# Decay sums by broadcast transfers and GpSimd masks instead of matmuls, in a two-layer SSD / RG-LRU trunk

## The chip, the cores and the metric

The kernel runs on one core of a Trainium2 chip. The metric is the device time of one execution in microseconds (us), as a median of several runs; lower is better. One of the executions is also profiled, and its trace is what the rows below are read from. Engines are named as the profile names them: PE is the matmul engine (PEld its weight loads), DVE the vector engine, ACT the scalar engine, POOL is GpSimd, and SP issues the transfers (DMAs).

## The reference, cut to what matters

Two layers, 256 tokens, width 2048. Layer 0 has an SSD mixer, layer 1 an RG-LRU mixer; each is followed by a SwiGLU block and a gated input block. The change is inside the SSD mixer: 64 heads in 8 groups, two chunks of 128 tokens.

```python
dt = softplus(dt + dt_bias)                 # (256, 64)
a_cs = cumsum(dt * a, within a chunk)       # the decay sums
seg = a_cs[l] - a_cs[s]
decay_in = exp(where(l >= s, seg, -inf))    # (128, 128) per head and chunk
cb = C @ B.T                                # per group and chunk
y_diag = (cb * decay_in) @ (xs * dt)
# the state that chunk 0 hands to chunk 1 adds
# C[l] . B[s] * exp(a_cs1[l] + a_cs0[end] - a_cs0[s]) for l in chunk 1, s in chunk 0
```

For each head the kernel needs three 128x128 blocks of exponentials: chunk 0 on itself, chunk 1 on chunk 0, and chunk 1 on itself. Row s of a block holds the sum at token l along the free axis, less the sum at s, and the two diagonal blocks are masked to l >= s.

## The kernel before, in words

All products run as split products in fp32r: a weight tile `raw` is split by ACT into `hi` (L238) and by DVE into `lo` (L239), and each activation tile holds its own hi and lo side by side in 512 columns. A **panel** (`panel`) makes 512 output rows in four PSUM banks: 16 k-steps, taken in four **quarters** of four k-steps. A quarter is 16 matmuls of 512 columns (L266, weight `hi`) and then 16 of 256 columns (L264, weight `lo`). One load of 512 KB brings two k-steps, so a panel has eight loads, issued by SP (L230) in program order into five `raw` buffers; `hi` and `lo` have four buffers each, so ACT and DVE work at most four loads ahead of PE.

Small work is written as generators that a panel advances while it goes: `post` by one step for each k-step, `side` by `pump` steps. The order in which instructions then stand on each engine is set at build time; nothing is chosen while the kernel runs.

The SSD mixer's panels stand in this order: 18, 19 (C), the rates' panel `w_dt` (one quarter's work: 16 hi and 16 lo), 16, 17 (B), 8 to 15 (the eight groups' xs), 0 to 7 (z). The normalizing factor `r` comes from `bc_part(2)` while panel 19 runs (L186, L212 on PE). `dt_part` computes softplus (L356 to L370, a chain on DVE), the sums `cs` by scans (L412), and four transposes of them (L423). `group(g)` runs while the next panel runs: scaled (L162), convolution (ACT L349, DVE L351) and SiLU to `xs`; the C-by-B product (L444, L445) and its copy `cm`; transposes of `xs` to `xdt` (L454, L456); then for each of 8 heads two matmuls that spread the masked sums over the partitions (L468 the mask, L470 the sums), two exponentials on ACT (called at L473 and L474, recorded under L98), a product with `cm` on DVE (L475); then 16 matmuls that give the outputs (L487, L489) and `y` (L493). GpSimd runs only in the setup (L80, L82).

Of the kernel before, what the change touches and what calls it, by code (L numbers as in the profile page):

```python
# [11 lines left out]
F32 = mybir.dt.float32  # L12
F32R = mybir.dt.float32r
I32 = mybir.dt.int32
AF = mybir.ActivationFunctionType
# [10 lines left out]
KG = 2  # L26
RUN = 16
# [15 lines left out]
class Trunk:  # L43
# [7 lines left out]
    def __init__(self, ctx, tc):  # L51
        self.tc, self.nc = tc, tc.nc
        nc = self.nc
        pool = lambda name, bufs, **kw: ctx.enter_context(tc.tile_pool(name=name, bufs=bufs, **kw))
        self.const = pool("const", 1)
        self.act = pool("act", 48)
        self.wraw = pool("wraw", 5)
        self.wsp = pool("wsp", 4)
        self.tmp = pool("tmp", 2)
        self.ssd = pool("ssd", 2)  # L60
        self.ps = pool("ps", 8, space=bass.MemoryType.PSUM)
# [8 lines left out]
        self.identr = c.tile([P, P], F32R, name="identr")  # L70
        nc.vector.tensor_copy(self.identr, self.ident)
        self.sel = c.tile([P, 64], F32R, name="sel")
        nc.vector.tensor_tensor(self.sel, self.ident[:, :64], self.ident[:, 64:], ALU.add)
# [5 lines left out]
        mask = self.act.tile([P, 256], F32, name="mask", tag="a")  # L79
        nc.gpsimd.memset(mask, 0.0)  # L80
        for o in (0, P):
            nc.gpsimd.affine_select(  # L82
                out=mask[:, o:o + P], in_=mask[:, o:o + P],
                compare_op=ALU.is_ge, fill=-1e30, base=0, pattern=[[1, P]], channel_multiplier=-1)
        self.mask = c.tile([P, 256], F32R, name="maskr")
        nc.vector.tensor_copy(self.mask, mask)
        self.vecs = c.tile([P, NVEC], F32, name="vecs")
        self.h = c.tile([P, KT, T], F32, name="h")
# [7 lines left out]
    def table(self, out, in_, func, **kw):  # L96

        i = self.nc.scalar.activation(out, in_, func, **kw).ins  # L98
        if self.last_table is not None:
            self.tc.add_manual_dep(  # L100
                i, self.last_table.name,
                mybir.DependencyInfo(mybir.DependencyClass.NoSync, mybir.DependencyReason.DATA),
                reason="table order")
        self.last_table = i

# [116 lines left out]
    def weights(self, w, width=PW, kt=KG, also=None, single=False):  # L222
# [6 lines left out]
        if not single:  # L229
            nc.sync.dma_start(raw, w)  # L230
# [142 lines left out]
    def ssd_mixer(self, w_dt, w_in, w_out, load):  # L373
# [5 lines left out]

        def conv_silu(j, t, out):  # L380
            c = self.tmp.tile([P, T], F32, name="c", tag="c", bufs=3)
            self.conv(t, "ssd_cw", "ssd_cb", 48, j, c)
            self.table(out, c, AF.Silu)
# [14 lines left out]
        def dt_part(t):  # L398
# [23 lines left out]
            for i, src in enumerate((dt[:, :P], dt[:, P:], cs[:, :P], cs[:, P:256])):  # L422
                nc.tensor.transpose(b[:, i * P:(i + 1) * P], src, self.ident)  # L423
# [4 lines left out]
            self.csr, self.dts, self.ncs = csr, dts, ncs  # L428
            yield

        def of0(t):

            return t[:, :384].rearrange("p (a b) -> p a b", a=3)[:, 0:3:2, :]

        def group(g, ts):
            xs = [self.act.tile([P, 2, T], F32, name=f"xs{i}", tag="a") for i in range(2)]
            xs = [t[:, i, :] for t in xs for i in range(2)]
            for j, t in enumerate(ts):
                conv_silu(g * NB + j, self.scaled(t, self.r), xs[j])
                yield  # L440
# [3 lines left out]
            nc.tensor.matmul(of0(b), bt[:, :P], ct, start=True, stop=True, skip_group_check=True)  # L444
            nc.tensor.matmul(b[:, P:256], bt[:, P:], ct[:, P:], start=False, stop=True, skip_group_check=True)  # L445
# [4 lines left out]
            for c in range(2):  # L450
                yield
# [8 lines left out]
            yield  # L460
            es = []

            def decays(j):

                for hh in range(2):
                    hd = g * 8 + j * 2 + hh
                    rb = self.bank()
                    nc.tensor.matmul(rb[:, :256], self.identr, self.mask, start=True, stop=False,  # L468
                                     skip_group_check=True)
                    nc.tensor.matmul(rb[:, :384], self.sel[:, hd:hd + 1].to_broadcast([P, P]), self.csr,  # L470
                                     start=False, stop=True, skip_group_check=True)
                    e = pool.tile([P, 384], F32, name="e", tag="e", bufs=12)
                    self.table(of0(e), of0(rb), AF.Exp, bias=self.ncs[:, 0, hd:hd + 1])  # L473
                    self.table(e[:, P:256], rb[:, P:256], AF.Exp, bias=self.ncs[:, 1, hd:hd + 1])  # L474
                    nc.vector.tensor_tensor(e, e, cm, ALU.mult)  # L475
                    es.append(e)
                    yield

            def outputs(j):

                yb = self.bank()
                for i in (j, j + 1):
                    for hh in range(2):
                        e = es[i * 2 + hh]
                        ch = slice(i * P + hh * 64, i * P + hh * 64 + 64)
                        o = yb[hh * 64:hh * 64 + 64, (i - j) * T:(i - j + 1) * T]
                        nc.tensor.matmul(o, xdt[0][:, ch], of0(e), start=i == j, stop=False,  # L487
                                         skip_group_check=True)
                        nc.tensor.matmul(o[:, P:256], xdt[1][:, ch], e[:, P:256], start=False, stop=True,  # L489
# [51 lines left out]
        for g in range(8):  # L541
            banks = self.panel(w_in[g], u)
            self.post.append(gated(g, self.totals(banks)))
# [292 lines left out]
```

## Time and profile before

| | before |
|---|---|
| median of 3 runs | 2688.74 us (2687.94 to 2689.76) |
| profiled execution, its own time | 2686.82 us |
| its span in the trace | 2685.0 us |
| PE busy | 2663.3 us (99%) |
| PEld busy | 2348.0 us (87%) |
| DVE busy | 1821.1 us (68%) |
| ACT busy | 1497.8 us (56%) |
| POOL busy | 1.4 us (0%) |
| granted PE clock, mean | 0.998 |

The profiled execution's own time is 1.8 us above its span and 1.9 us below the median. Matmuls are pipelined, so the busy time of one is longer than the distance to the next; the distance between starts is what a matmul costs. The eight groups' stretch lies between about 132 and 360 us of the span.

### The profile page before, as it was taken

The page shows a single profiled execution, that of the slowest core. Times are in us where ns is not written, and L with a number is a line of the kernel's source. Part 1 is how long each engine was busy: PE and PEld are TensorE (multiplying, and loading weights), DVE is VectorE, ACT ScalarE, POOL GpSimd, SP SyncE. Part 2 cuts the span into 40 slices and gives each one's busy share as a digit, 9 for nine tenths or more (in the row PEclk, how much of TensorE's full clock was granted, in tenths as well). Part 3 has the DMA queues.
Part 4 walks back from the last instruction along what each step waited for, and adds up shares of the span by engine and source line. Part 5 has one row for each costly group of instructions (what it writes and reads, how often), then busy time and mean ns, then how long its engine had stood idle before and what let it go on. Part 6 is the DMA issues. An engine that isn't in the chain of part 4 may idle for free.

```text
span 2685.0 us, 40694 instructions
## 1 busy us (share of the span) xinstructions
PE 2663.3 (99%) x15474; PEld 2348.0 (87%) x15474; DVE 1821.1 (68%) x3101; ACT 1497.8 (56%) x2399; POOL 1.4 (0%) x9
## 2 busy tenths in 40 slices
PE   9999999999999999999999999999999999999998
PEld 7888888888888888888888888888888888888887
DVE  8888788855565555555666899977666555665667
ACT  7677666644444444444455678856444444444555
POOL 0000000000000000000000000000000000000000
PEclk9999999999999999999999999999999999999999
DMA  6544455555555555555555556555555555556553
GB/s 234 187 157 145 139 170 181 182 190 184 193 189 189 189 187 188 195 190 189 194 187 184 185 181 195 183 187 197 189 188 188 192 190 184 189 192 199 186 187 127
DMA packets 137140, 495.24 MB, mean 184 GB/s; under 512 B 15344, under 2 KB 15728, under 8 KB 136944
## 3 DMA queue, kind: packets, MB, share of 16 engines
q1 hardware_dynamic: 136944, 492.65, 55.5%
q8 instruction: 121, 1.98, 0.3%
q14 instruction: 75, 0.61, 0.1%
HBM read 490.49 MB, written 2.10 MB: 183 GB/s over the span
## 4 chain that ended last, share of the span: by engine, by line
PE 95%; DVE 3%; ACT 1%; issue 0%; DMA 0%; SPq 0%; DVEq 0%; ACTq 0%
PE bank L266 60%; PE bank L264 31%; DVE lo L239 1%; PE bank L487 1%; PE bank L581 1%; DVE c L351 0%; PE bank L470 0%; ACT hi L238 0%; PE bank L454 0%; PE bank L468 0%; DVE t L155 0%; PE bank L583 0%; PE bank L489 0%; DMA raw<-in_w_ssd_in_dram 0%; DVE xc L351 0%
## 5 line engine op out<-in xcount | busy, mean ns | idle before, releaser
L266 PE MATMUL bank<-x,hi 128*128 128x512 f32 x7360 | 1776.1, 392 | 6.3 <-ACT hi L238 5.5
L266 PEld LDWEIGHTS bank<-x,hi 128*128 128x128 f32 x7360 | 1350.8, 189 | 266.1 <-ACT hi L238 6.4
L238 ACT CAST hi<-raw 128x1024 fp32r<-128x1024 f32 (+1 forms) x932 | 973.0, 1048 | 1035.5 <-PE bank L266 984.6
L239 DVE TENSOR_TENSOR lo<-raw,hi 128x1024 fp32r<-128x1024 f32 (+1 forms) x932 | 1108.1, 1220 | 506.1 <-issue 419.6
L264 PEld LDWEIGHTS bank<-x,lo 128*128 128x128 f32 x7360 | 950.1, 191 | 39.5 <-DVE lo L239 2.5
L264 PE MATMUL bank<-x,lo 128*128 128x256 f32 x7360 | 969.7, 283 | 1.7 <-DVE lo L239 1.6
L155 DVE TENSOR_TENSOR t<-bank,s 128x256 f32<-128x256 f32 x448 | 161.7, 418 | 294.5 <-ACT s L152 294.2
L152 ACT COPY s<-bank 128x256 f32<-128x256 f32 x496 | 160.1, 374 | 12.6 <-PE bank L583 5.5
L162 DVE TENSOR_TENSOR t<-t,r 128x256 f32<-128x256 f32 x216 | 81.4, 420 | 0.0
L351 DVE SCALAR_TENSOR_TENSOR c<-t,vecs,c 128x255 f32<-128x255 f32 (+2 forms) x144 | 61.7, 481 | 1.3 <-ACT c L349 1.3
L144 ACT ACTIVATE x<-h,vecs 128x256 fp32r<-128x256 f32 x96 | 47.4, 501 | 16.8 <-DVE h L332 13.8
L98 ACT ACT_TABLE_LOAD x41 | 52.6, 1283 | 4.6 <-DVE c L351 4.0
L332 DVE TENSOR_TENSOR h<-h,t 128x256 f32<-128x256 f32 x144 | 54.2, 421 | 0.2
L145 DVE SCALAR_TENSOR_TENSOR x<-h,vecs,x 128x256 fp32r<-128x256 f32 x96 | 45.6, 481 | 5.6 <-ACT x L144 5.6
L98 ACT ACTIVATE e<-bank,ncs 128x256 f32<-128x256 f32 (+1 forms) x128 | 44.4, 423 | 5.9 <-PE bank L470 5.3
L175 DVE TENSOR_TENSOR acc<-acc,q 128x256 f32<-128x256 f32 x104 | 43.8, 421 | 3.1 <-ACT q L168 1.8
L168 ACT ACTIVATE q<-h 128x256 f32<-128x256 f32 x104 | 41.5, 405 | 5.6 <-DVE h L332 3.8
L98 ACT ACTIVATE sg<-t 128x256 f32<-128x256 f32 x88 | 32.3, 413 | 18.7 <-DVE t L162 18.7
L136 ACT CAST x<-t 128x256 fp32r<-128x256 f32 x88 | 31.8, 403 | 18.7 <-DVE t L673 18.7
L475 DVE TENSOR_TENSOR e<-e,cm 128x384 f32<-128x384 f32 x64 | 33.4, 554 | 3.7 <-ACT e L98 3.6
L349 ACT ACTIVATE c<-t,vecs 128x256 f32<-128x256 f32 x48 | 26.4, 592 | 13.2 <-DVE t L162 13.1
L137 DVE TENSOR_TENSOR x<-t,x 128x256 fp32r<-128x256 f32 x88 | 33.3, 421 | 0.0
(129 smaller groups left out, 719.5 us busy)
## 6 DMA issues: line engine op xcount, KB each, us to landing
raw<-in_w_ffn_in_dram SPq DMA_DIRECT2D x352, 512.0 KB, 4.4
raw<-in_w_ffn_out_dram SPq DMA_DIRECT2D x176, 512.0 KB, 4.4
raw<-in_w_ssd_in_dram SPq DMA_DIRECT2D x158, 512.0 KB, 4.3
raw<-in_w_ssd_out_dram SPq DMA_DIRECT2D x64, 512.0 KB, 4.4
raw<-in_w_ple_gate_dram SPq DMA_DIRECT2D x64, 512.0 KB, 4.2
raw<-in_w_lru_in_dram SPq DMA_DIRECT2D x64, 512.0 KB, 4.4
raw<-in_w_lru_out_dram SPq DMA_DIRECT2D x32, 512.0 KB, 4.4
raw<-in_w_ple_up_dram SPq DMA_DIRECT2D x8, 512.0 KB, 4.9
```

Of the source, the lines that this page charges most:

```text
L98: i = self.nc.scalar.activation(out, in_, func, **kw).ins
L144: nc.scalar.activation(x[:, :T], src, AF.Copy, scale=w)
L145: nc.vector.scalar_tensor_tensor(x[:, T:], src, w, x[:, :T].bitcast(F32), ALU.mult, ALU.subtract)
L152: nc.scalar.copy(s, b[:, T:])
L155: nc.vector.tensor_tensor(t, b[:, :T], s, ALU.add)
L162: self.nc.vector.tensor_tensor(t, t, r, ALU.mult)
L238: self.last_hi = nc.scalar.copy(hi, src).ins
L239: nc.vector.tensor_tensor(lo, src, hi.bitcast(F32), ALU.subtract)
L264: nc.tensor.matmul(b[:, T:], wt, x[:, :T], start=False, stop=k == nk - 1, skip_group_check=True)
L266: nc.tensor.matmul(b, wt, x, start=k == 0, stop=False, skip_group_check=True)
L332: self.nc.vector.tensor_tensor(hb, hb, t, ALU.add)
L351: nc.vector.scalar_tensor_tensor(out[:, d:], t[:, :T - d], self.vec(cw, (3 - d) * ntap + i), out[:, d:], ALU.mult, ALU.add)
```

## The change

The matmuls that spread the sums over partitions go, with the constants made for them (`identr`, `sel`, `mask`, `csr`). In their place the sums `cs` of all heads are written once to DRAM in 8 copies (`sums`), and for each pair of heads one transfer reads 768 values of a copy into all 128 partitions of a tile `e` (16 partitions read the same copy). Two GpSimd instructions then put -1e30 where l < s in the diagonal blocks, and the exponentials run in place on that tile. `move` puts each of these transfers into SP's queue behind the weight load issued last. One product with `cm` covers two heads. The three blocks of a head lie in another order in the tile. The rates' panel runs second instead of third, `dt_part` is pumped at 0.6 instead of 0.3, and a group's exponentials for two pairs of heads are written ahead of the transposes.

```diff
+    def move(self, out, in_):
+        i = self.nc.sync.dma_start(out, in_).ins
+        self.tc.add_manual_dep(
+            i, self.last_load.name, ...,
+            reason="place in the queue")
...
-            nc.sync.dma_start(raw, w)
+            self.last_load = nc.sync.dma_start(raw, w).ins
...
+        sums = self.dram.tile([NCOPY, 64, 384], F32, name="sums")
...
-            for c in range(2):
-                nc.vector.tensor_tensor_scan(cs[:, c * P:(c + 1) * P], self.ones, adt[:, c * P:(c + 1) * P],
+            for c, o in ((0, 0), (1, 256)):
+                nc.vector.tensor_tensor_scan(cs[:, o:o + P], self.ones, adt[:, c * P:(c + 1) * P],
                                              0.0, ALU.mult, ALU.add)
-            nc.vector.tensor_scalar(cs[:, 256:], cs[:, P:256], cs[:, P - 1:P], None, ALU.add)
-            csr = pool.tile([P, 384], F32R, name="csr", tag="csr", bufs=1)
-            nc.scalar.copy(csr, cs)
-            nc.vector.tensor_tensor(csr[64:, :], cs[64:, :], csr[64:, :].bitcast(F32), ALU.subtract)
+            nc.vector.tensor_scalar(cs[:, P:256], cs[:, 256:], cs[:, P - 1:P], None, ALU.add)
...
+            self.move(sums.rearrange("n h c -> h n c"), cs[:64].unsqueeze(1).to_broadcast([64, NCOPY, 384]))
+            yield
...
             for j, t in enumerate(ts):
                 conv_silu(g * NB + j, self.scaled(t, self.r), xs[j])
+                e = pool.tile([P, 2, 384], F32, name="e", tag="e", bufs=8)
+                hd = g * 8 + 2 * j
+                src = sums[0, hd:hd + 2, :]
+                self.move(e.rearrange("p h c -> p (h c)"),
+                          bass.AP(src.tensor, src.offset, [[64 * 384, NCOPY], [0, P // NCOPY], [1, 768]]))
+                for o in (0, 256):
+                    nc.gpsimd.affine_select(
+                        out=e[:, :, o:o + P], in_=e[:, :, o:o + P], compare_op=ALU.is_ge, fill=-1e30,
+                        base=0, pattern=[[0, 2], [1, P]], channel_multiplier=-1)
+                es.append(e)
                 yield
...
+            def decays(j):
+                e = es[j]
+                for hh in range(2):
+                    hd = g * 8 + j * 2 + hh
+                    self.table(e[:, hh, :256], e[:, hh, :256], AF.Exp, bias=self.ncs[:, 0, hd:hd + 1])
+                    self.table(e[:, hh, 256:], e[:, hh, 256:], AF.Exp, bias=self.ncs[:, 1, hd:hd + 1])
+                    yield
+                nc.vector.tensor_tensor(e, e, cm.unsqueeze(1).to_broadcast([P, 2, 384]), ALU.mult)
...
-                for hh in range(2):
-                    hd = g * 8 + j * 2 + hh
-                    rb = self.bank()
-                    nc.tensor.matmul(rb[:, :256], self.identr, self.mask, start=True, stop=False,
-                                     skip_group_check=True)
-                    nc.tensor.matmul(rb[:, :384], self.sel[:, hd:hd + 1].to_broadcast([P, P]), self.csr,
-                                     start=False, stop=True, skip_group_check=True)
-                    e = pool.tile([P, 384], F32, name="e", tag="e", bufs=12)
-                    self.table(of0(e), of0(rb), AF.Exp, bias=self.ncs[:, 0, hd:hd + 1])
-                    self.table(e[:, P:256], rb[:, P:256], AF.Exp, bias=self.ncs[:, 1, hd:hd + 1])
-                    nc.vector.tensor_tensor(e, e, cm, ALU.mult)
...
             yield from decays(0)
             yield from decays(1)
+            tokens(0)
             yield from decays(2)
+            tokens(1)
             yield from decays(3)
+            yield
             yield
...
         ts = self.totals(self.panel(w_in[18], u, pre=load))
         self.post.append(bc_part(2, ts, self.last_hi))
+        dt = self.totals(self.panel(w_dt, u, kt=8, nb=1, post=False))
         ts = self.totals(self.panel(w_in[19], u))
         self.post.append(bc_part(3, ts))
-        ts = self.totals(self.panel(w_dt, u, kt=8, nb=1, post=False))
-        self.side.append(dt_part(ts[0]))
+        self.side.append(dt_part(dt[0]))
         for n in (0, 1):
-            ts = self.totals(self.panel(w_in[16 + n], u, pump=0.3))
+            ts = self.totals(self.panel(w_in[16 + n], u, pump=0.6))
```

How the instructions stand is shown at three places. First PE where the rates' transposes stand, before. The L266 and L264 rows are quarters of panels 16 and 17; `sp` is the softplus result.

```order
L266 MATMUL bank<-x,hi 128x512 x16
L264 MATMUL bank<-x,lo 128x256 x16
L266 MATMUL bank<-x,hi 128x512 x16
L264 MATMUL bank<-x,lo 128x256 x16
L423 MATMUL bank<-ident,sp_779 128x128 x2
L423 MATMUL bank<-ident,cs 128x128 x2
L266 MATMUL bank<-x,hi 128x512 x16
```

And the same place on PE after (the lines of the panel are L263 and L261 now, of the transposes L419):

```order
L263 MATMUL bank<-x,hi 128x512 x16
L261 MATMUL bank<-x,lo 128x256 x16
L419 MATMUL bank<-ident,sp_753 128x128 x2
L263 MATMUL bank<-x,hi 128x512 x3
L419 MATMUL bank<-ident,cs 128x128 x2
L263 MATMUL bank<-x,hi 128x512 x13
L261 MATMUL bank<-x,lo 128x256 x16
```

Before, the four transposes stood behind the first quarter of panel 17; now those of `sp` stand straight behind the last quarter of panel 16 and those of `cs` three matmuls later, one quarter earlier. The transposes that spread `r` stand behind four lo matmuls of panel 19's third quarter in both.

Second, PE in a group (group 1 of 8), before, from the C-by-B product to the first heads:

```order
L444 MATMUL bank<-bc_106,bc_102 128x2x128
L445 MATMUL bank<-bc_106,bc_102 128x128
L266 MATMUL bank<-x,hi 128x512 x6
L454 MATMUL bank<-ident,xs_2113 128x128 x2
L266 MATMUL bank<-x,hi 128x512 x4
L454 MATMUL bank<-ident,xs_2114 128x128
L266 MATMUL bank<-x,hi 128x512 x2
L454 MATMUL bank<-ident,xs_2113 128x128 x2
L454 MATMUL bank<-ident,xs_2114 128x128
L266 MATMUL bank<-x,hi 128x512 x4
L264 MATMUL bank<-x,lo 128x256 x4
L468 MATMUL bank<-maskr,identr 128x256
```

And after:

```order
L450 MATMUL bank<-bc_94,bc_90 128x256
L451 MATMUL bank<-bc_94,bc_90 128x128
L263 MATMUL bank<-x,hi 128x512 x16
L261 MATMUL bank<-x,lo 128x256 x16
L471 MATMUL bank<-ident,xs_2092 128x128 x2
L471 MATMUL bank<-ident,xs_2093 128x128 x2
```

The pairs of L468 and L470 are gone; the transposes stand behind the whole second quarter, a further four behind six matmuls of the third, and the 16 output matmuls behind the third quarter.

Third, SP's queue from the last of panel 18's loads to the second group, after:

```order
L227 DMA raw<-in_w_dt_dram 128x1024 x2
L227 DMA raw<-in_w_ssd_in_dram 128x1024 x23
L97 DMA sums<-cs 64x8x384
L227 DMA raw<-in_w_ssd_in_dram 128x1024 x11
L97 DMA e<-sums 128x1x768 x4
L227 DMA raw<-in_w_ssd_in_dram 128x1024 x8
L97 DMA e<-sums 128x1x768 x4
```

Before, 144 weight loads stood in one row there. Now the write of `sums` stands ahead of panel 17's last load, and each group's four reads stand together between the second and the third load of a panel.

## Rows read from the trace of the kernel before

**Rows 1.** The page's chain that ended last: shares of the span by engine.

```profile
PE 95%; DVE 3%; ACT 1%; issue 0%; DMA 0%; SPq 0%; DVEq 0%; ACTq 0%
```

**Rows 2.** Groups of PE instructions, 131 to 360 us: busy, mean ns, idle before.

```profile
L470 PE MATMUL bank<-csr,sel 128*128 128x384 f32 x64 | 21.1, 338 | 0.0
```

**Rows 3.** Timeline of PE in one group: start us, us, instructions.

```profile
191.92 0.60 PE L444 MATMUL bank<-bc,bc 128*128 128x256 f32 x2
...
199.75 1.09 PE L266 MATMUL bank<-x,hi 128*128 128x512 f32 x4
...
204.71 0.64 PE L264 MATMUL bank<-x,lo 128*128 128x256 f32 x4
205.18 0.28 PE L468 MATMUL bank<-maskr,identr 128*128 128x256 f32 x1
...
205.47 1.59 PE L264 MATMUL bank<-x,lo 128*128 128x256 f32 x12
...
208.65 0.66 PE L487 MATMUL bank<-e,xdt 128*64 128x256 f32 x4
...
211.45 2.60 PE L266 MATMUL bank<-x,hi 128*128 128x512 f32 x10
...
215.79 3.82 PE L266 MATMUL bank<-x,hi 128*128 128x512 f32 x16
219.45 2.08 PE L264 MATMUL bank<-x,lo 128*128 128x256 f32 x16
221.36 0.60 PE L444 MATMUL bank<-bc,bc 128*128 128x256 f32 x2
```

**Rows 4.** Timeline of PE before the groups.

```profile
45.83 0.38 PE L212 MATMUL bank<-ident,rs_y 128*128 128x128 f32 x2
...
75.71 1.22 PE L264 MATMUL bank<-x,lo 128*128 128x256 f32 x8 [1.19 <-DVE lo L239]
...
82.34 3.82 PE L266 MATMUL bank<-x,hi 128*128 128x512 f32 x16
```

**Rows 5.** Timeline of DVE before the groups; in brackets idle time before, and its end.

```profile
47.93 1.43 DVE L162 TENSOR_TENSOR t<-t,r 128x256 f32<-128x256 f32 x4
...
54.91 1.27 DVE L351 SCALAR_TENSOR_TENSOR c<-t,vecs,c 128x255 f32<-128x255 f32 x3 [1.25 <-ACT c L349]
...
82.86 0.42 DVE L155 TENSOR_TENSOR t<-bank,s 128x256 f32<-128x256 f32 x1 [0.92 <-ACT s L152]
...
84.40 0.42 DVE L370 TENSOR_TENSOR sp<-sp,sp 128x256 f32<-128x256 f32 x1
```

**Rows 6.** Timeline of DVE in the group of rows 3.

```profile
198.81 1.23 DVE L239 TENSOR_TENSOR lo<-raw,hi 128x1024 fp32r<-128x1024 f32 x1 [0.73 <-ACT xs L98]
199.95 1.28 DVE L456 TENSOR_TENSOR xdt<-bank,dts 128x512 f32<-128x512 f32 x2
201.15 1.49 DVE L475 TENSOR_TENSOR e<-e,cm 128x384 f32<-128x384 f32 x3
202.55 1.22 DVE L239 TENSOR_TENSOR lo<-raw,hi 128x1024 fp32r<-128x1024 f32 x1
```

**Rows 7.** Timeline of ACT in the group of rows 3.

```profile
198.17 0.41 ACT L98 ACTIVATE xs<-c 128x256 f32<-128x256 f32 x1
...
199.90 2.88 ACT L98 ACTIVATE e<-bank,ncs 128x256 f32<-128x256 f32 x8
202.67 1.05 ACT L238 CAST hi<-raw 128x1024 fp32r<-128x1024 f32 x1
```

**Rows 8.** One line's instructions, GpSimd's masks: ns min/median/max, first and last start.

```profile
L82 POOL TENSOR_SCALAR_AFFINE_SELECT mask<-mask x2: 292/292/292, 1.5 to 1.7; 128x128 f32<-128x128 f32 x2
```

**Rows 9.** Busy us by engine in one stretch: PE, PEld, DVE, ACT, POOL; clock, DMA, GB/s.

```profile
190.00:220.00 30.00, 30.00 (x194) 26.04 (x193) 24.18 (x44) 21.62 (x41) 0.00 (x0) 1.00 0.43 141
```

**Rows 10.** The page's DMA queue: packets, MB, share of 16 engines.

```profile
q1 hardware_dynamic: 136944, 492.65, 55.5%
```

**Rows 11.** What SP's queue waited for, 131 to 360 us: us, times, longest.

```profile
SPq L230 <- DVE lo L239: 218.4, 65, 13.4
```

More of the change, by code (lines that the diff above doesn't have):

```diff
@@ L26 @@
 KG = 2
+NCOPY = 8
 RUN = 16
@@ L60, in __init__ @@
         self.ssd = pool("ssd", 2)
+        self.dram = pool("dram", 1, space=bass.MemoryType.DRAM)
         self.ps = pool("ps", 8, space=bass.MemoryType.PSUM)
@@ L69, in __init__ @@
         make_identity(nc, self.ident)
[L70 to L73, printed above, removed]
         self.ones = c.tile([P, P], F32, name="ones")
@@ L77, in __init__ @@
         nc.scalar.activation(self.warm, self.ones[:, :1], AF.Identity)
[L79 to L86, printed above, removed]
         self.vecs = c.tile([P, NVEC], F32, name="vecs")
@@ L104, in table @@
         self.last_table = i
+    def move(self, out, in_):
+        i = self.nc.sync.dma_start(out, in_).ins
+        self.tc.add_manual_dep(
+            i, self.last_load.name,
+            mybir.DependencyInfo(mybir.DependencyClass.NoSync, mybir.DependencyReason.DATA),
+            reason="place in the queue")
     def bank(self):
@@ L421, in dt_part @@
             b = self.bank()
-            for i, src in enumerate((dt[:, :P], dt[:, P:], cs[:, :P], cs[:, P:256])):
+            for i, src in enumerate((dt[:, :P], dt[:, P:], cs[:, :P], cs[:, 256:])):
                 nc.tensor.transpose(b[:, i * P:(i + 1) * P], src, self.ident)
@@ L427, in dt_part @@
             nc.vector.tensor_scalar(ncs, b[:, 256:], -1.0, None, ALU.mult)
-            self.csr, self.dts, self.ncs = csr, dts, ncs
+            self.dts, self.ncs = dts, ncs
             yield
-        def of0(t):
-            return t[:, :384].rearrange("p (a b) -> p a b", a=3)[:, 0:3:2, :]
+            self.move(sums.rearrange("n h c -> h n c"), cs[:64].unsqueeze(1).to_broadcast([64, NCOPY, 384]))
+            yield
         def group(g, ts):
@@ L437, in group @@
             xs = [t[:, i, :] for t in xs for i in range(2)]
+            es = []
             for j, t in enumerate(ts):
                 conv_silu(g * NB + j, self.scaled(t, self.r), xs[j])
+                e = pool.tile([P, 2, 384], F32, name="e", tag="e", bufs=8)
[8 more added lines that the diff above has]
+                es.append(e)
                 yield
@@ L443, in group @@
             bt, ct = bc[g // 2][:, g % 2, :], bc[4 + g // 2][:, g % 2, :]
-            nc.tensor.matmul(of0(b), bt[:, :P], ct, start=True, stop=True, skip_group_check=True)
-            nc.tensor.matmul(b[:, P:256], bt[:, P:], ct[:, P:], start=False, stop=True, skip_group_check=True)
+            nc.tensor.matmul(b[:, :256], bt[:, :P], ct, start=True, stop=True, skip_group_check=True)
+            nc.tensor.matmul(b[:, 256:384], bt[:, P:], ct[:, P:], start=False, stop=True, skip_group_check=True)
             cm = pool.tile([P, 384], F32, name="cm", tag="cm")
@@ L449, in group, with tokens @@
             yield
-            for c in range(2):
-                yield
+            def decays(j):
[6 more added lines that the diff above has]
+                nc.vector.tensor_tensor(e, e, cm.unsqueeze(1).to_broadcast([P, 2, 384]), ALU.mult)
+            def tokens(c):
                 b = self.bank()
@@ L459, in group @@
                 xdt.append(x)
-            yield
-            es = []
-            def decays(j):
-                for hh in range(2):
-                    hd = g * 8 + j * 2 + hh
-                    rb = self.bank()
-                    nc.tensor.matmul(rb[:, :256], self.identr, self.mask, start=True, stop=False,
-                                     skip_group_check=True)
-                    nc.tensor.matmul(rb[:, :384], self.sel[:, hd:hd + 1].to_broadcast([P, P]), self.csr,
-                                     start=False, stop=True, skip_group_check=True)
-                    e = pool.tile([P, 384], F32, name="e", tag="e", bufs=12)
-                    self.table(of0(e), of0(rb), AF.Exp, bias=self.ncs[:, 0, hd:hd + 1])
-                    self.table(e[:, P:256], rb[:, P:256], AF.Exp, bias=self.ncs[:, 1, hd:hd + 1])
-                    nc.vector.tensor_tensor(e, e, cm, ALU.mult)
-                    es.append(e)
-                    yield
             def outputs(j):
@@ L483, in outputs @@
                     for hh in range(2):
-                        e = es[i * 2 + hh]
+                        e = es[i][:, hh, :]
                         ch = slice(i * P + hh * 64, i * P + hh * 64 + 64)
                         o = yb[hh * 64:hh * 64 + 64, (i - j) * T:(i - j + 1) * T]
-                        nc.tensor.matmul(o, xdt[0][:, ch], of0(e), start=i == j, stop=False,
+                        nc.tensor.matmul(o, xdt[0][:, ch], e[:, :256], start=i == j, stop=False,
                                          skip_group_check=True)
-                        nc.tensor.matmul(o[:, P:256], xdt[1][:, ch], e[:, P:256], start=False, stop=True,
+                        nc.tensor.matmul(o[:, P:256], xdt[1][:, ch], e[:, 256:], start=False, stop=True,
                                          skip_group_check=True)
@@ L541, in ssd_mixer @@
         for g in range(8):
-            banks = self.panel(w_in[g], u)
-            self.post.append(gated(g, self.totals(banks)))
+            ts = self.totals(self.panel(w_in[g], u))
+            self.post.append(gated(g, ts))
         self.out_product(w_out, yn, "norm_ffn", 0)
```

## The prediction

> **What bounds the kernel now.** The chain that ended last is PE for 95% of the span [rows 1], so I first looked for where PE waits, and then for what each engine does in the groups' stretch, since that is where the change works. The matmuls that go had no idle time in front of them [rows 2]: PE ran through them one after the other, so their time is PE's own and not time in which it would have waited anyway. The timeline of PE gives the prices, as distances between starts. A quarter of a panel is 16 hi matmuls in 219.45 - 215.79 = 3.66 us and 16 lo in 221.36 - 219.45 = 1.91 us, 5.57 together; one group, from one C-by-B product to the next, takes 221.36 - 191.92 = 29.44 us [rows 3]. Before the groups there is one wait of PE, 1.19 us for a `lo` of DVE [rows 4]; DVE is the engine with little to spare there, and with 24.18 us busy in 30 it is the second busiest in the groups too [rows 9].
>
> **The matmuls that go.** There are 64 pairs of L468 and L470, one for each head [rows 2]. A pair among lo matmuls took 205.47 - 205.18 = 0.29 us [rows 3]. Among hi matmuls, a quarter's 16 took 204.71 - 199.75 = 4.96 us with four pairs between them, so a pair cost (4.96 - 3.66)/4 = 0.325 us [rows 3]. That gives 64 x 0.29 = 18.6 us or 64 x 0.325 = 20.8 us. I take 18.6, the clean stretch. As PE never waited there, all of it comes off the path, unless a wait takes its place.
>
> **Where a wait can take its place in a group.** Two results reach PE in the group. I count from the C-by-B product, at 191.92 in the rows. First, the transposes of `xs`. The last `xs` was ready at 198.17 + 0.41, that is 6.66 us in [rows 7], and what stands ahead of it on ACT and DVE is the same after. PE now reaches the transposes after the product (0.60) and one quarter (5.57), 6.2 us in, and has the first ones to do: a wait of about 0.3 us. Second, the products of the last pair of heads, which the outputs need. Exponentials start 199.90 - 191.92 = 8.0 us in, and eight take 202.67 - 199.90 = 2.77 us [rows 7]; after, all sixteen stand together, since nothing of PE is waited for between them, and end 13.5 us in. The weight cast that stood after the eighth now stands behind the sixteenth; at most four loads are split ahead, some 11 us of PE's work, so that cast has cover. The product with `cm` took (202.55 - 201.15)/3 = 0.47 us for 384 columns, and a `lo` of 1024 columns 199.95 - 198.81 = 1.14 us [rows 6], so one of 768 columns is an estimated 0.87 us, and the last ends 14.4 us in. PE gets to the outputs after the `xs` wait, eight transposes (0.6) and another quarter, about 12.8 us in; the outputs take 211.45 - 208.65 = 2.80 us [rows 3] and the last pair stands in their last quarter, 14.9 us in. That is half a microsecond of slack, on which GpSimd's masks can draw. The masks of the next group run while this group's products do. Two follow each transfer, and a 128x128 mask took 0.29 us [rows 8], so one of twice the elements is between 0.29 and 0.58 us; if both hold DVE up ahead of the last product it is 1.16 us late, and PE waits about 0.7 us more. I take 0.5 us a group in all (0.3 for the transposes, 0.2 of collisions), 8 x 0.5 = 4.0 us, with ends of 0 and 1.0, that is 0 and 8 us.
>
> **The rates' panel second.** `r` is spread by PE four lo matmuls into the third quarter of panel 19, before and after. Panel 19 now starts one quarter later, so this moves from 45.83 [rows 4] to 51.4 us. DVE's first product with `r` came 47.93 - 45.83 = 2.1 us behind it [rows 5], with one `lo` of 1.14 us between that now stands ahead; so it starts at about 52.4. From there to the end of softplus DVE took 84.82 - 47.93 = 36.9 us [rows 5]. By the order, 8 `lo` stand in this stretch after, where 11 stood (3.4 us less), and one total less (0.3). The two idle times of 1.25 and 0.92 us [rows 5] can close. So softplus ends between 52.4 + 31.0 = 83.4 and 85.6 us. Its transposes used to stand a quarter behind panel 16; now they stand straight behind it, and PE gets there at 82.34 - 1.19 = 81.15 us [rows 4], for the `lo` that it waited 1.19 us for now stands ahead of softplus's reciprocal. PE waits 2.3 to 4.5 us. The sums `cs` come one `lo` and six short instructions later (1.14 + 6 x 0.3, as four L162 take 1.43 us [rows 5]), 3.0 us; PE has 3 matmuls and 2 transposes to do meanwhile, some 0.85 us, and waits 2.1 us again. Less the 1.19 us that goes, the move costs 3.2 to 5.4 us. I take 3.5: DVE carries a backlog there and should have no idle time left. What is queued behind those transposes on PE is panel 17 itself, so nothing hides this.
>
> **What costs nothing.** The write of `sums` stands in SP's queue ahead of one weight load and waits for `cs`; that load waits for a `lo` that stands behind `cs` on DVE anyway. The reads of `e` wait for buffers used two groups before. SP waits for DVE's `lo` 65 times, 218.4 us in all [rows 11], so issuing 32 more transfers takes only its waiting time. DVE loses 64 products of 0.47 us and gets 32 of 0.87, 0.3 us less a group; the exponentials stay as many, of the same sizes. The constants of the setup go, where PE waits for transfers.
>
> **The sum.** -18.6 + 4.0 + 3.5 = -11.1 us. On the profiled execution, 2686.82 us for a span of 2685.0, that is 2675.7; it lay 1.9 us under the median, so the median goes from 2688.74 to 2677.6 us. With the ends of the terms it is -20.8 + 0 + 3.2 = -17.6 (2671) to -18.6 + 8 + 5.4 = -5.2 (2683.5).
>
> **Rivals.**
>
> All of it hides. If DVE is faster through softplus than counted and the groups have no wait, 18.6 to 20.8 us go: 2668 to 2670, say 2669. For it: outputs and exponentials are within half a microsecond. Against it: softplus is a chain on a DVE without idle time.
>
> GpSimd holds DVE up all the time. DVE has 24.18/30 x 29.44 - 0.3 = 23.4 us of work a group [rows 9]. If every mask of length m blocks it for its whole length, it has 23.4 + 8m; PE's group after is 29.44 - 8 x 0.29 + 0.5 = 27.6. At m = 0.58, the upper end of [rows 8], DVE sets 28.0 us a group: 8 x (29.44 - 28.0) - 3.5 = 8 us less, 2681. No trace here has a mask running beside DVE.
> The Trainium skill says in "SBUF — State Buffer", section "Who interferes with whom", that a DVE instruction with two SBUF inputs contends with a GpSimd instruction that reads SBUF, and the second to issue waits for the whole of the first. By that rule this rival holds; no run here shows it yet.
>
> The slower side is the same mechanism with longer masks. The mask here is of another shape (two pieces of 128), and its length is not in the trace; at m = 1.0 us DVE has 31.4 us a group, 8 x 2.0 + 3.5 = 19 us more: 2708. It makes the kernel slower from 8 x (23.4 + 8m - 29.44) + 3.5 > 0 on, that is m over 0.70 us, if all of it blocks.
>
> The transfers delay the weights. The queue's 492.65 MB took 55.5% of 16 engines' 2685 us, so one engine moves 20.7 KB a microsecond [rows 10]. The four tiles of a group, 393 KB each, take 4.7 us on 16 engines and 9.5 us on 8. The three weight loads behind them in SP's queue are then 5 or 9 us late. Five buffers of 29.44/8 = 3.7 us each give some 18 us between issue and use, less the landing and the wait for a buffer, so the first case is covered and the second is at the edge. If the loads miss it by an estimated 1.2 us a group, the cast on ACT is late, with it the copies behind it, the convolution and the transposes: 8 x 1.2 = 9.6 us, 2687.
> The Trainium skill says in "DMA: Bandwidth & Descriptors", section "Rules for kernel authors", that an outermost dimension of size c below 16 confines a transfer to at most c engines. The diff's read has 8 outermost, so by that rule it is the 9.5 us; no row here has such a transfer.
>
> That the matmuls would stay is no rival: the order shows them gone.
>
> **How the numbers follow.** The forecast of 2677.6 gets 0.50; all hidden (2669) 0.18; masks holding DVE (2681) 0.08; weights delayed (2687) 0.14; long masks (2708) 0.10. What a measurement can tell from no change is 0.2%, 5.4 us, so faster is below 2683.4: 0.50 + 0.18 + 0.08 = 0.76; within 0.2% 0.14; slower 0.10. The range from 2668 to 2687 leaves out the long masks, part of the delayed weights and the edge of the hidden case.
>
> **What would show it.** Right: PE's matmul count falls by 128 and a group's period to about 27.6 us; PE waits of 2 to 5 us at L419 for DVE, near 81 to 87 us, and the old wait at 75 us gone; small waits of PE at L471 for ACT; none at the outputs above 0.5 us. Wrong: PE waits at L486 for DVE's products, DVE's idle time gone in the groups or its `lo` longer than 1.23 us beside POOL (masks); masks over 0.7 us; ACT's cast waiting for a weight load in the groups (transfers); no wait at L419 (all hidden). A drop of the granted clock around the wait at 81 us would add to it, and I have not counted one.

## The result, and the profile after

The changed kernel takes 2726.07 us (median of 4 runs, 2724.03 to 2732.37) where the kernel before takes 2688.42 us (2687.94 to 2689.76, 4 runs beside them): a ratio of 1.0145, 95% interval 1.0132 to 1.0157. It is 37.6 us slower. The forecast was 2677.6 us, and its range ended at 2687. In the profiled executions the span went from 2685.0 to 2723.4 us, 38.4 us more.

The chain that ended last, by engine, and the queue of the loads (packets, MB, share of 16 engines), from the page of the changed kernel; they answer to [rows 1] and [rows 10]:

```profile
PE 84%; DVE 7%; DMA 6%; ACT 2%; issue 1%; SPq 1%; DVEq 0%; ACTq 0%
...
q1 hardware_dynamic: 141824, 506.02, 57.9%
```

DMA had 0% of the chain before and has 6% now, DVE 7% instead of 3%. The queue carries only 13 MB more. The matmuls are 128 fewer, as the diff says. What PE waits for between 60 and 402 us, the whole stretch in which the change can act (us in total, times, longest):

```profile
PE bank L471 <- ACT xs L87: 18.7, 12, 2.8
PE bank L450 <- DVE t L152: 10.3, 3, 5.2
PE bank L261 <- DVE lo L236: 5.0, 5, 1.6
PE bank L419 <- DVE sp L367: 3.4, 1, 3.4
```

These are 37.4 us. The kernel before had one wait there, the 1.19 us of [rows 4]. Busy time by engine in some stretches of the changed kernel (PE, PEld, DVE, ACT, POOL; then granted clock, DMA share, GB/s):

```profile
85.00:110.00 25.00, 23.46 (x117) 19.78 (x118) 19.56 (x35) 13.47 (x20) 0.00 (x0) 0.87 0.74 228
131.00:160.00 29.00, 23.85 (x124) 20.67 (x122) 16.98 (x30) 16.85 (x35) 2.31 (x6) 0.88 0.56 158
160.00:190.00 30.00, 23.02 (x137) 19.32 (x136) 16.13 (x30) 13.82 (x22) 3.60 (x8) 0.94 0.67 151
190.00:220.00 30.00, 28.94 (x168) 24.78 (x168) 21.52 (x36) 20.02 (x38) 5.26 (x8) 0.89 0.65 177
400.00:430.00 30.00, 30.00 (x179) 26.63 (x178) 25.76 (x59) 21.04 (x41) 0.00 (x0) 1.00 0.50 161
```

Against 190 to 220 us of before [rows 9], PE is no longer full, the granted clock is 0.89 instead of 1.00, and DVE and ACT do less, not more. After 400 us, where the groups are done, PE is full at a clock of 1.00 again. The trace's clock record has eight stretches at 1.2 GHz between 80 and 402 us, 41.0 us together. PE waits for 4.2 us of that anyway; in the other 36.8 us half speed loses up to 18.4 us. The kernel before has no such stretch there.

So the account of the span is -18.6 (the pairs that went) + 37.4 - 1.2 (waits of PE) + 18.4 (clock) = +36.0 us, of 38.4 measured; 2.4 us have no row. The gain is there; the waits and the clock behind them took it back almost three times over.

**Where the waits come from.** What ACT waited for in the groups, first the changed kernel (131 to 400 us), then the kernel before (131 to 365 us):

```profile
ACT hi L235 <- DMA raw<-in_w_ssd_in_dram: 70.7, 17, 14.3
```

```profile
ACT hi L238 <- PE bank L266: 52.8, 30, 5.0
```

Before, the cast of a weight load waited for PE to free a buffer: the loads were ahead. Now it waits for the load. The chain from 185 to 215 us shows why (start us, us, what):

```profile
190.42 0.59 SPq L97
...
191.12 0.59 SPq L97
...
191.80 0.58 SPq L97
...
192.48 0.58 SPq L97
...
193.16 0.86 SPq L227
...
194.12 16.16 DMA raw<-in_w_ssd_in_dram
...
210.38 1.05 ACT hi L235
211.43 0.28 ACT s L149
211.73 1.42 DVE t L152 x4
```

SP issues the four reads of decay sums and then weight loads. The load that the chain follows was issued at 194.12 and landed 16.16 us later. Its cast (`hi`) stands in ACT's order ahead of the copies `s` of the panel's totals; so the copies, the totals `t`, the convolution and `xs` on DVE and ACT are all late. A `lo` that stands among them frees the buffer for SP's next load, and SP issues the next reads and the loads after them behind that: the chain has the same pieces every 31 to 37 us, each with 15.5 to 20.9 us of a load in flight. The masks show when the four reads landed (GpSimd's timeline; idle before, and its end):

```profile
198.21 1.89 POOL L442 TENSOR_SCALAR_AFFINE_SELECT e<-e 128x256 f32<-128x256 f32 x2 [21.16 <-DMA e<-sums]
202.17 0.77 POOL L442 TENSOR_SCALAR_AFFINE_SELECT e<-e 128x256 f32<-128x256 f32 x2 [2.07 <-DMA e<-sums]
205.35 1.83 POOL L442 TENSOR_SCALAR_AFFINE_SELECT e<-e 128x256 f32<-128x256 f32 x2 [2.41 <-DMA e<-sums]
```

One tile lands every 3 to 4 us. By the trace's records of packets, a group's four reads are 512 packets of 3 KB at 0.205 us each, and they keep eight of the 16 engines busy (8.5 at most in any microsecond of this group). The columns are those above; in the first row packets of reads and of weights move, in the second of reads alone, in the third of weights alone:

```profile
199.00:200.00 1.00, 1.00 (x10) 1.00 (x9) 1.00 (x2) 1.00 (x3) 1.00 (x2) 1.00 1.08 213
...
204.00:205.00 1.00, 1.00 (x5) 0.82 (x5) 1.00 (x3) 0.00 (x0) 0.00 (x0) 1.00 0.52 187
...
210.00:211.00 1.00, 1.00 (x6) 0.83 (x5) 0.00 (x0) 0.83 (x2) 0.00 (x0) 1.00 0.52 213
```

From 196 to 202 us the packets of the reads keep 8.3 to 8.5 engines busy and those of the weight loads behind them 8.1 to 8.3; from 203 to 205 no weight packet moves, though the load issued at 194.12 has not landed; its last packets move when the reads are done. So half of a load's packets stand behind the reads. 512 x 0.205 / 8 = 13.1 us: that is what a weight load behind the reads has ahead of it on eight of its engines.
The Trainium skill's "DMA: Bandwidth & Descriptors", section "Rules for kernel authors", says that an outermost dimension below 16 holds a transfer to at most so many engines; the trace agrees, with 8 outermost and 8.5 engines at most.

PE pays at the C-by-B product (L450), which waits for the totals `t`, and at the transposes of `xs` (L471), and then once more by its clock. PE's timeline:

```profile
180.30 1.22 PE L450 MATMUL bank<-bc,bc 128*128 128x256 f32 x2 [5.17 <-DVE t L152]
181.31 0.64 PE L451 MATMUL bank<-bc,bc 128*128 128x128 f32 x2
181.60 4.91 PE L263 MATMUL bank<-x,hi 128*128 128x512 f32 x16
186.52 0.73 PE L261 MATMUL bank<-x,lo 128*128 128x256 f32 x4
187.10 0.40 PE L471 MATMUL bank<-ident,xs 128*128 128x128 f32 x2
189.29 0.33 PE L471 MATMUL bank<-ident,xs 128*128 128x128 f32 x1 [1.79 <-ACT xs L87]
```

Sixteen hi matmuls took 4.91 us behind the 5.17 us wait, where they take 3.82 at 2.4 GHz [rows 3]; the clock record has 1.2 GHz there up to 183.7 us.

### The profile page after: what moved, and what is told of

It is laid out like the page before. It is cut to its first block, busy times and chain, and to the rows that moved or that the text cites. A ratio compares the mean times of both kernels' runs of the same rounds, so it can differ in the third digit from the quotient of the medians.

```text
span 2723.4 us, 40676 instructions
## 1 busy us (share of the span) xinstructions
PE 2664.6 (98%) x15346; PEld 2344.1 (86%) x15346; DVE 1817.8 (67%) x3065; ACT 1500.3 (55%) x2398; POOL 37.6 (1%) x70
## 4 chain that ended last, share of the span: by engine, by line
PE 84%; DVE 7%; DMA 6%; ACT 2%; issue 1%; SPq 1%; DVEq 0%; ACTq 0%
PE bank L263 55%; PE bank L261 28%; DMA raw<-in_w_ssd_in_dram 5%; DVE lo L236 2%; DVE c L348 1%; DVE t L152 1%; ACT hi L235 1%; DVE t L159 1%; DVE xc L348 0%; PE bank L583 0%; SPq L97 0%; ACT s L149 0%; ACT L87 0%; DVE hs L616 0%; PE bank L585 0%
## 5 line engine op out<-in xcount | busy, mean ns | idle before, releaser
L263 PE MATMUL bank<-x,hi 128*128 128x512 f32 x7360 | 1780.3, 393 | 7.9 <-ACT hi L235 5.6
L263 PEld LDWEIGHTS bank<-x,hi 128*128 128x128 f32 x7360 | 1359.3, 190 | 274.4 <-ACT hi L235 7.3
L261 PEld LDWEIGHTS bank<-x,lo 128*128 128x128 f32 x7360 | 949.9, 191 | 44.0 <-DVE lo L236 7.5
L261 PE MATMUL bank<-x,lo 128*128 128x256 f32 x7360 | 969.6, 283 | 5.0 <-DVE lo L236 5.0
L87 ACT ACTIVATE e<-e,ncs 128x256 f32<-128x256 f32 (+1 forms) x128 | 45.2, 442 | 0.1
L442 POOL TENSOR_SCALAR_AFFINE_SELECT e<-e 128x256 f32<-128x256 f32 x64 | 36.9, 599 | 330.4 <-DMA e<-sums 279.3
L465 DVE TENSOR_TENSOR e<-e,cm 128x768 f32<-128x768 f32 x32 | 30.6, 989 | 4.2 <-ACT e L87 3.4
```

The lines of the kernel that those rows point to most:

```text
L261: nc.tensor.matmul(b[:, T:], wt, x[:, :T], start=False, stop=k == nk - 1, skip_group_check=True)
L263: nc.tensor.matmul(b, wt, x, start=k == 0, stop=False, skip_group_check=True)
```

## The experiments

Theory A: the reads run on 8 engines and, in one queue with the weights, make these late. Theory B: the new order of the work is at fault. Theory C: the rates' panel in second place costs its own wait and clock. All ratios are to the kernel before, measured beside each on the same chip, with 95% intervals.

**Sixteen copies.** One constant:

```diff
-NCOPY = 8
+NCOPY = 16
```

Expected: 

> Sixteen copies of the sums instead of eight, nothing else changed: the outermost dimension of every read of decay sums goes from 8 to 16. Theory A (the eight-engine reads hold up the weights): in the changed kernel the 512 packets of a group's four reads took 0.205 us each on 8 engines, 13.1 us, and the weight load issued behind them landed 15 to 17 us after its issue. On 16 engines they should take 6.6 to 7.5 us, the load behind them should land in 9 to 11 us, and most of the 32.6 us that PE waits between 125 and 402 us, with the six stretches at half clock behind those waits (34 us at 1.2 GHz, some 15 us lost), should go: 2675 to 2695 us. Theory B (the new order is at fault: exponentials ahead of the transposes, masks on GpSimd): the waits for xs at the transposes stay, and the time stays within 8 us of 2726 us.

Measured: 2678.67 us, 0.9967 (0.9954 to 0.9980): 47 us less for one constant. What PE still waits for, 60 to 402 us:

```profile
PE bank L471 <- ACT xs L87: 3.4, 4, 1.4
PE bank L419 <- DVE sp L367: 3.3, 1, 3.3
PE bank L261 <- DVE lo L236: 1.4, 2, 1.1
```

Of 32.6 us of waits in the groups the 3.4 at the transposes are left (those for `lo` lie at 70 and 82 us, ahead of the groups), and of the seven stretches at 1.2 GHz in the groups (34.1 us) none is left, only the one behind the rates' transposes. A group's reads took 7.2 to 8.9 us. Theory A stands, B falls.

**No reads.** The masks and the exponentials take a resident tile (`still`); the write of the sums goes too, so the decays hold no sums.

```diff
-                self.move(e.rearrange("p h c -> p (h c)"), bass.AP(...))
...
-                        out=e[:, :, o:o + P], in_=e[:, :, o:o + P], ...
+                        out=e[:, :, o:o + P], in_=self.still.rearrange("p (h c) -> p h c", h=2), ...
...
-                    self.table(e[:, hh, :256], e[:, hh, :256], AF.Exp, ...)
+                    self.table(e[:, hh, :256], self.still, AF.Exp, ...)
```

Expected: 

> The changed kernel without the write of the sums and without the 32 reads: masks and exponentials take a resident tile of one value, at the same sizes and in the same places. It leaves out the sums in the decays. Theory A: without the reads the weights land as in the kernel before, the group waits and the half-clock stretches go, and what is left is the gain of 64 pairs against the early wait: 2670 to 2680 us. Theory B: the order is at fault and the waits for xs at the transposes stay: 2705 to 2726 us.

Measured: 2674.25 us, 0.9951 (0.9936 to 0.9966), and no wait of PE in the groups at all. With masks and exponentials in the changed kernel's places, it was the transfers that made PE wait; and not the write of the sums, for sixteen copies double it and most of the waits go.

**One copy, on 16 and on 8 engines.** The first experiment changed the number of copies and the outermost dimension together. These two part them:

```diff
-NCOPY = 8
+NCOPY = 1
...
-    bass.AP(src.tensor, src.offset, [[64 * 384, NCOPY], [0, P // NCOPY], [1, 768]])
+    bass.AP(src.tensor, src.offset, [[0, P], [1, 768]])
```

and, for the second, `[[0, 8], [0, 16], [1, 768]]` in that place.

Expected of 128 outermost: 

> The changed kernel with one copy of the sums, and every read with 128 as its outermost dimension, all of them from the same 3 KB of DRAM. If the outermost dimension alone decides how many DMA engines carry a read, the reads run on 16 engines and the time is that of sixteen copies: 2677 to 2681 us. If 16 engines reading one place of DRAM hinder each other, a packet of 3 KB takes well above 0.205 us, and the time lies between 2685 and 2726 us.

Expected of 8 outermost: 

> One copy of the sums, but the read's outermost dimension is 8 again (8 by 16 repeats of the same 3 KB): it parts the number of DMA engines from the number of copies, which the run with sixteen copies changed together. Theory A (the count of engines does the harm): the four reads of a group keep 8 engines busy for some 9 us (512 packets of 0.14 us, the length with one copy, over 8), the loads behind them are late, and the waits at the groups come back in part: 2685 to 2705 us. Rival G (the eight separate copies did the harm, by their longer packets, and not the 8 engines): 2675 to 2680 us, as with one copy on 16.

Measured: 2676.19 us, 0.9955 (0.9938 to 0.9972), with 128 outermost, just under what I expected, and 2725.95 us, 1.0140 (1.0126 to 1.0154), with 8. The second is slower than I expected (2685 to 2705), since its packets took 0.21 us like those of eight copies, not the 0.14 us of one copy on 16 engines. Its waits of PE, 60 to 402 us:

```profile
PE bank L471 <- ACT xs L87: 20.0, 12, 2.8
PE bank L450 <- DVE t L152: 9.9, 3, 4.4
PE bank L261 <- DVE lo L236: 7.3, 9, 1.6
PE bank L419 <- DVE sp L367: 3.4, 1, 3.4
```

They are at the changed kernel's places, for about the same times. The same bytes from the same place cost 50 us more when the pattern begins with 8: of the two it is the count of engines, and the copies in DRAM, which the change made eight of, buy nothing here.

**The reads in ACT's queue.** Eight copies and eight engines, but not in the weights' queue:

```diff
-                self.move(e.rearrange("p h c -> p (h c)"),
+                nc.scalar.dma_start(e.rearrange("p h c -> p (h c)"),
```

Expected: 

> The changed kernel with its eight copies, but the 32 reads are issued by ACT, in ACT's own queue, and not by SP between the weight loads. The reads stay on 8 engines. Theory A1 (the harm is the order in one queue: on those 8 engines the weights' packets stand behind the reads' packets): the weight loads no longer wait behind four reads, the waits at the groups go, 32 issues of about 0.6 us fall on ACT (2.4 us a group, which it has free): 2676 to 2692 us. Theory A2 (8 engines have too little throughput for what they must carry, in whatever order): the waits stay, 2710 to 2726 us.

Measured: 2688.07 us (2684.36 to 2696.32, 10 runs), 1.0002 (0.9992 to 1.0011). Within the range of A1, far from A2:

```profile
PE bank L471 <- ACT xs L87: 6.8, 5, 2.9
PE bank L419 <- DVE sp L367: 3.4, 1, 3.4
PE bank L261 <- DVE lo L236: 2.3, 3, 1.1
```

The waits at L450 are gone, with the reads still on 8 engines, and ACT's wait for weight loads falls from 70.7 to 7.8 us (131 to 400 us). So 8 engines alone don't do the harm; it takes the reads ahead of the loads in one queue. How much of the 38 us is the queue and how much the time isn't parted: without `move` the reads are also issued earlier, from 95.7 us instead of 120.4, and a group's four over 4 to 17 us, where SP took 2 to 3. Some 9 us against sixteen copies remain, and these runs spread more than the others.

**The rates' panel: place and pace.** The change moves the panel and also raises the pace of the side work in the two panels behind it. I took back the place in the changed kernel:

```diff
-        dt = self.totals(self.panel(w_dt, u, kt=8, nb=1, post=False))
         ts = self.totals(self.panel(w_in[19], u))
         self.post.append(bc_part(3, ts))
+        dt = self.totals(self.panel(w_dt, u, kt=8, nb=1, post=False))
```

Then I put the second place into the kernel before by the reverse of this, once with the pace, which is the next two lines, and once without:

```diff
-            ts = self.totals(self.panel(w_in[16 + n], u, pump=0.3))
+            ts = self.totals(self.panel(w_in[16 + n], u, pump=0.6))
```

Expected, place taken back: 

> The rates' panel back in third place, the rest as in the changed kernel. Theory C (the second place costs its own wait and a stretch at half clock): the 3.39 us wait at the rates' transposes goes and the 6.8 us at 1.2 GHz behind it (3.4 us lost) with it, the old wait of 1.2 us at 75 us returns: 5 to 6 us less, 2720 to 2721 us. Rival D (the sums are then written later, so that the first group's reads and masks come too late): the wait moves to the first group, and the time is 2726 us or more.

Expected, before with both: 

> The kernel before with one edit: the rates' panel second, with the same faster pumping of the side work as in the changed kernel. Theory C: PE waits some 3.4 us at the rates' transposes and the granted clock falls to 1.2 GHz for about 6.8 us there, less the old wait of 1.2 us: 2693 to 2695 us. Rival (the place of the panel costs nothing by itself): 2687 to 2690 us.

Expected, before with the place alone: 

> The kernel before with the rates' panel second and the old pace of 0.3: the place alone, without the pace. Theory E: no wait for the softplus and no stretch at half clock, 2687 to 2690 us. Rival C: about as with both edits, 2693 to 2695 us.

Measured: 2723.00 us, 1.0133 (1.0116 to 1.0150), with the place taken back: its interval overlaps the changed kernel's, and the wait at L419 stayed, 3.4 us long, 1.8 us earlier. So the trace takes the cause away from the place. The kernel before went to 2694.32 us, 1.0024 (1.0014 to 1.0034), with both, and to 2690.27 us, 1.0010 (1.0001 to 1.0019), with the place alone, just above the range of theory E. Waits of PE, 60 to 402 us, in these two:

```profile
PE bank L423 <- DVE sp L370: 3.3, 1, 3.3
PE bank L264 <- DVE lo L239: 1.4, 2, 1.1
```

```profile
PE bank L264 <- DVE lo L239: 3.2, 4, 1.6
PE bank L423 <- DVE cs L412: 0.3, 1, 0.3
```

The pace brings the rates' transposes to PE before softplus is done, and the clock falls behind that wait (0.88 from 85 to 110 us, against 1.00 with the place alone): 4 us. The place costs some 2 us more, in four small waits for `lo`.

**Sixteen copies at the old pace.**

```diff
-NCOPY = 8
+NCOPY = 16
...
-            ts = self.totals(self.panel(w_in[16 + n], u, pump=0.6))
+            ts = self.totals(self.panel(w_in[16 + n], u, pump=0.3))
```

Expected: 

> Sixteen copies, and the side work of the two panels after the rates pumped at 0.3 a step as in the kernel before, instead of 0.6; the rates' panel stays second. Theory E (the early wait comes from the pace of the side work, which brings the rates' transposes in front of the third panel's casts, and not from the panel's place): the 3.3 us wait for the softplus goes, and the 6.8 us at 1.2 GHz behind it (3.4 us lost) with it: 2671 to 2674 us against 2678.7 us with sixteen copies alone. Rival C (the panel's place is at fault): the wait only moves, and the time stays at 2677 to 2681 us. Rival F (slower pumping makes the sums late): a wait at the first group's decays, above 2680 us.

Measured: 2674.61 us, 0.9951 (0.9936 to 0.9966), 4 us less than with sixteen copies alone and just above what I expected. The 3.3 us wait is down to 0.2, and the clock record has no stretch at 1.2 GHz in the panels. Five waits for `lo`, 3.1 us together, are left, four of them ahead of the groups: most of that is the price of the place. Two at the transposes, 2.0 us, are left too.

**The order.** One copy on 16 engines, with the transposes ahead of the exponentials again:

```diff
-            yield from decays(0)
-            yield from decays(1)
-            tokens(0)
-            yield from decays(2)
-            tokens(1)
-            yield from decays(3)
-            yield
+            for c in range(2):
+                yield
+                tokens(c)
             yield
+            for j in range(NB):
+                yield from decays(j)
```

Expected: 

> One copy on 16 engines, with the transposes of xs ahead of the exponentials again, in the slots of the kernel before: it takes back the order alone. Theory H (the order moves work that nobody waits for once the transfers land in time): 2674 to 2678 us, as with one copy. Rival (the order saves the waits for xs at the transposes, as it was meant to, or brings DVE's products in front of the casts): PE waits up to 0.8 us more or less in each group, 2670 to 2683 us.

Measured: 2675.97 us, 0.9954 (0.9940 to 0.9967), against 2676.19 with the change's order. The order is worth nothing either way.

**All that was learned, together.** One copy with 128 outermost, the rates' panel third and the old pace; masks, order and the missing pairs as in the change.

Expected: 

> One copy on 16 engines, the rates' panel third and the side work behind it pumped at 0.3, both as in the kernel before. By the theories that stand so far the early waits of 4.2 us and the stretch at half clock behind them (3.4 us lost) go, and 1.4 us of older waits stay: 2676.2 less 7.6 us, 2667 to 2671 us. Rival: as with sixteen copies at 0.3, small waits for the casts take the place of the one that goes, 2672 to 2676 us.

Measured: 2668.58 us (2668.31 to 2670.15), 0.9927 (0.9914 to 0.9941), 5 runs. It beats both kernels, the one before by 20 us. PE's waits, 60 to 402 us, and three groups on PE's timeline:

```profile
PE bank L261 <- DVE lo L236: 1.2, 1, 1.2
```

```profile
186.99 0.60 PE L450 MATMUL bank<-bc,bc 128*128 128x256 f32 x2
213.97 0.60 PE L450 MATMUL bank<-bc,bc 128*128 128x256 f32 x2
241.01 0.60 PE L450 MATMUL bank<-bc,bc 128*128 128x256 f32 x2
```

From the third on a group takes 26.98 to 27.04 us, against 29.44 of before [rows 3], and the only wait is the old one of [rows 4].

## Why the prediction was wrong, point by point

- **The matmuls that go: right.** 18.6 us was taken. The best version's span is 2666.5 against 2685.0, 18.5 us less, with the same single wait of 1.2 us in both.
- **Waits in a group: mis-sized, for another cause.** The forecast had 0.5 us a group, from the order at the transposes and from collisions at the outputs. With the reads on 16 engines and the rates as before there is none, and the group is 29.44 - 8 x 0.29 = 27.1 us, as the pairs alone make it. In the changed kernel the waits are 32.6 us between 125 and 402 us, 4.1 a group, at the transposes and at the C-by-B product, which was not named; they come from the loads. At the outputs PE doesn't wait, as forecast.
- **What costs nothing: this step failed.** "Issuing 32 more transfers takes only SP's waiting time" is true of the issues, 0.59 us each. It says nothing of what the transfers do in the queue behind them. I priced the issue and not the queue: the load that the chain follows behind a group's reads took 15.5 to 20.9 us to land, and ACT's casts waited 70.7 us for loads, which is the sign that the prediction gave for this rival.
- **The rival of delayed weights: right mechanism, wrong sizes.** It had the 8 engines, the late cast, the copies behind it and the transposes. Three terms were too small. The reads: 9.5 us at 20.7 KB a microsecond and engine; the trace has 13.1 us of packets and bursts of 12.9 to 17.8 us, for a packet of 3 KB took 0.205 us, 15 KB a microsecond. The slack: I counted five buffers of 3.7 us as some 18 us; but a load is issued only when a `lo` of DVE frees its buffer, and 16 us in flight used it up. The feedback: late loads delay `lo`, which delays the issue of the next reads and loads, so the waits are 4.1 us a group and not the 1.2 that I had estimated. That it got 0.14 and ended at 2687 put the result outside the range.
- **The clock: left out.** The text named it as uncounted. Of the 54.6 us that the account finds lost (36.2 + 18.4), up to 18.4 are matmuls at 1.2 GHz behind the waits. In the runs here in which PE waits 3.3 us or more at the rates' transposes, a stretch at half speed follows, of 6.8 us (3.4 with the panel third in the changed kernel); the runs without that wait have none there.
- **The rates' panel: size right, reason wrong in part.** The wait at L419 is 3.39 us, at 83.1 to 86.5 us, inside the forecast's 2.3 to 4.5. The second wait, for `cs`, isn't in the trace; the old 1.19 us didn't go but moved, as 1.10 at 70 us and 0.26 at 82 us. 3.39 + 1.10 + 0.26 - 1.19 = 3.56, by luck the 3.5 taken; the wait for `cs` was also worked out with 0.3 us for an instruction where 1.43/4 is 0.36. But the clock added up to 2.5 us (6.8 us at half speed, of which PE waited 1.8), and the pace of 0.6 causes the wait, not the place.
- **GpSimd's masks: the rival fell.** Masks have a median of 0.408 us, inside the 0.29 to 0.58 forecast, but a mean of 0.599 and a longest of 1.468; so the sign "masks over 0.7 us" came without the harm. In the best version the mean is 0.684 us, and PE doesn't wait. One line's instructions there (ns min/median/max), masks, then the products with `cm`, then `lo`:

```profile
L442 POOL TENSOR_SCALAR_AFFINE_SELECT e<-e x64: 400/406/1387, 121.7 to 312.3; 128x256 f32<-128x256 f32 x64
```

```profile
L465 DVE TENSOR_TENSOR e<-e,cm x32: 947/959/1208, 141.6 to 336.0; 128x768 f32<-128x768 f32 x32
```

```profile
L236 DVE TENSOR_TENSOR lo<-raw,hi x72: 1208/1217/1425, 133.9 to 364.5; 128x1024 fp32r<-128x1024 f32 x72
```

It is mostly the masks that grow, to three times their length, while DVE's instructions grow by about a quarter at most. At the median length the rival's formula gives DVE 23.4 + 8 x 0.406 = 26.6 us a group, under the 27.0 measured, so the period can't tell. The lengths can: the 53 DVE instructions that ran beside a mask there are 2.9 us longer in all than the medians of their kinds, 0.4 us a group, where masks that block for their whole length would cost 3.2.
The Trainium skill ("SBUF — State Buffer", section "Who interferes with whom") calls the ports that DVE and GpSimd share an exclusive lock and lets issue order decide who blocks; the trace agrees in that both sides grew, 24 masks by up to 0.98 us and 19 DVE instructions by up to 0.25 us.

## What to carry to other kernels

A transfer added to a queue of loads costs what it does to the loads behind it: ask on how many DMA engines its access pattern lets it run, multiply its packets out over those, and set that against the time that the loads really have in hand, which is read from what their consumers wait for and not from the number of buffers. A read that repeats a row over the partitions does better with the 128 repeats as its first dimension than with a few copies. And once a full PE starts to wait for microseconds, price its clock too: here 36 us more of waits cost some 55.

## What the runs showed of the hardware that I had not expected

- Reading one place 128 times over is not slower than reading copies: a 3 KB packet took 0.14 us from one copy and 0.19 us from sixteen, both on 16 engines (2676.19 and 2678.67 us, with ratios whose intervals overlap). With 8 engines it took 0.21 us from one copy and from eight. The weights beside it are part of that: in the changed kernel it took 0.157 us with no weight packet in flight and 0.228 us with seven to nine. They don't explain the difference on 16 engines, which with no weight packet in flight is 0.139 against 0.185 us; its cause is open.
- The same transfers, on 8 engines again, cost 38 us less from ACT's queue, where they are also issued earlier, than from SP's (2688.07 against 2726.07).
- Beside DVE, a GpSimd mask of 0.40 us took up to 1.47 us, and DVE's instructions grew by at most 0.25 us.
